# The first mixer's depthwise convolution: 32x32 products on four PSUM banks in place of 64x64 products on two

## The chip, the core and the metric

The kernel runs on one core of a Trainium2 chip. The core has a matrix engine (TensorE, PE in the rows), a vector engine (VectorE, DVE), a scalar engine (ScalarE, ACT), GpSimd (POOL, hardly used here) and SyncE (SP), whose queue issues nearly all transfers. TensorE writes into PSUM, eight banks of 128 partitions x 512 fp32 numbers; everything else lives in SBUF, with 128 partitions, or in DRAM. The metric is the time of one execution on the device in microseconds (us), lower is better.

## The reference, cut to what matters

Two residual layers and their feed-forward networks on 1024 tokens of width 1024. The first layer's mixer ("mixer 0") has two parallel parts behind one input projection: a gated depthwise causal convolution of 31 taps on 512 channels, and an mLSTM with four heads of width 128.

```python
z = h @ w_in                                   # ca, cg, q, k, v, og, gates
u = ca * jax.nn.sigmoid(cg)
u = causal_depthwise_conv(u, conv_w, conv_b)   # 31 taps, each channel by itself
u = jax.nn.silu(layernorm(u, ln_g, ln_b))
...                                            # mLSTM on q, k, v -> hm
return jnp.concatenate([u, hm], -1) @ w_out
```

Everything is float32. The large projections are done as three products of numbers split in a high and a low part; the convolution and the mLSTM use plain fp32 products, each of which the profile shows as two records.

## The kernel before, in words

**The convolution on TensorE.** The 512 channels come in four blocks of 128; block i is made by `conv_in(i)` (gate, line 378 and on) and convolved by `conv(i)` (line 393 and on). A time t is written as 8n + s: s is a phase (8 of them), n runs over 128. `conv_in` leaves u as (channel, phase, n) and stores it to DRAM (`ud[i]`, L391). `conv` loads it back with (channel, phase) on the partitions (tile `ur`, L399), with four columns of zeros ahead of n = 0 (L397). One output phase of one channel is then a sum over the 8 input phases and over five shifts of n. So a product has 8 channels x 8 phases = 64 rows, the same 64 as outputs, and 128 columns (n), and five of them (m = 0..4) add up in PSUM. The band matrices (tile `cw`, L405) are prepared on the host and are mostly zeros: 8 channels do not mix.

Sixteen blocks of 8 channels by five shifts are 80 products for each `conv(i)`. Two row halves (j: partitions 0 to 63 and 64 to 127) go to two banks, two column halves (hc) to the halves of a bank's partitions; e picks the bank's columns and the band tile. When all are done, VectorE adds the bias and moves the banks to SBUF (L417, two instructions of 512 columns).

**What surrounds it.** The mixer's program is written in the order of `ORDER0` (line 31): c0 g0 c1 c2 q0 c3 a0a v0 x0a v1 x0b g1 q1 a1a v2 x1a v3 x1b and so on. c is `conv_in`, v is `conv`, g a head's v and output gate projection (`head_vo`, its products are L174 to L176 into tile `mm`, 128x256), q a head's q and k projection (`head_qk`), a and x the mLSTM of a head in two halves of 512 tokens (`head_pre`: L595 to L609; `head_mix`: L627 to L649). A list scheduler moves instructions from this order: on each engine it takes, by priority, what is ready in its own model of time. Each engine then executes its list strictly in that order.

**PSUM.** Four banks have the tag "mm" (projections), four the tag "sm" (convolution, mLSTM, sums). A tag's banks go round in the order in which tiles are asked for in the program.

**Weights.** `weights()` (L164 to L168) loads a projection's matrix as `raw` (two buffers), rounds it on ScalarE to `wH` (L167) and takes the rest on VectorE to `wL` (L168). `wH` and `wL` have three buffers each, and the band tiles `cw` take turns in the same ones. Tile `ur` has one buffer: the load for one `conv` starts when the `conv` before it has done all its products.

## Time and profile before

| | |
|---|---|
| median of 3 runs | 2102.48 us (2101.52 to 2103.54) |
| profiled execution | 2098.65 us, span 2096.9 us |
| granted TensorE clock over the span | 0.999 |
| TensorE busy | 2076.3 us, 99% |
| VectorE, ScalarE busy | 1507.4 us (72%), 865.5 us (41%) |
| the four bursts of convolution products (L411) | from 148.89, 163.00 (two records of it at 162.00), 212.50 and 226.80 us |

How rows are read: a row of the timeline is the start in us, the length, the engine (PEld is the weight load that overlaps PE), the line, the operation, the tiles written and read, the shapes, and a count of instructions that were merged; in square brackets stands how long the engine was idle just before and what ended it. A row of windows is a stretch, its length, then for each engine its busy time and the number of instructions in the stretch, the granted clock and the share and rate of the DMA engines. "Stand" below is time in which TensorE has nothing that it may start.

### The profile page before, as it was taken

The page shows a single profiled execution, that of the slowest core. Times are in us where ns is not written, and L with a number is a line of the kernel's source. Part 1 is how long each engine was busy: PE and PEld are TensorE (multiplying, and loading weights), DVE is VectorE, ACT ScalarE, POOL GpSimd, SP SyncE. Part 2 cuts the span into 40 slices and gives each one's busy share as a digit, 9 for nine tenths or more (in the row PEclk, how much of TensorE's full clock was granted, in tenths as well). Part 3 has the DMA queues.
Part 4 walks back from the last instruction along what each step waited for, and adds up shares of the span by engine and source line. Part 5 has one row for each costly group of instructions (what it writes and reads, how often), then busy time and mean ns, then how long its engine had stood idle before and what let it go on. Part 6 is the DMA issues. An engine that isn't in the chain of part 4 may idle for free.

```text
span 2096.9 us, 28455 instructions
## 1 busy us (share of the span) xinstructions
PE 2076.3 (99%) x10687; PEld 1753.5 (84%) x10687; DVE 1507.4 (72%) x2292; ACT 865.5 (41%) x1411; POOL 2.9 (0%) x15
## 2 busy tenths in 40 slices
PE   9999999999999999999999999999999999999998
PEld 8889988888888888888899978888888888888887
DVE  7555798777776666877865677667877666677686
ACT  6212337453222222444645546644522222235553
POOL 0000000000000000000000000000000000000000
PEclk9999999999999999999999999999999999999999
DMA  4323353654443334735436543553544333374344
GB/s 163 91 97 101 107 131 121 212 183 165 164 146 102 110 102 148 270 101 148 147 125 235 195 141 119 173 191 136 196 163 163 112 115 100 102 282 136 100 126 147
DMA packets 152590, 307.36 MB, mean 147 GB/s; under 512 B 24128, under 2 KB 37312, under 8 KB 152448
## 3 DMA queue, kind: packets, MB, share of 16 engines
q1 hardware_dynamic: 152176, 305.24, 44.2%
q8 instruction: 85, 1.39, 0.3%
q14 instruction: 57, 0.47, 0.1%
q10 hardware_dynamic: 272, 0.26, 0.0%
HBM read 224.67 MB, written 80.77 MB: 146 GB/s over the span
## 4 chain that ended last, share of the span: by engine, by line
PE 95%; DVE 2%; ACT 2%; DMA 1%; issue 0%; SPq 0%; DVEq 0%; ACTq 0%
PE mm L175 20%; PE mm L174 20%; PE mm L176 20%; PE sm L176 10%; PE sm L174 10%; PE sm L175 10%; PE sm L1270 1%; PE sm L1269 1%; PE sm L1272 1%; DVE wL L168 0%; DVE bs L1057 0%; DMA rb<-rowd 0%; PE sm L1297 0%; PE sm L1258 0%; PE sm L630 0%
## 5 line engine op out<-in xcount | busy, mean ns | idle before, releaser
L175 PE MATMUL mm<-hL,wH 128*128 128x512 f32 x1356 | 530.9, 392 | 0.5 <-DVE hL L339 0.4
L176 PE MATMUL mm<-hH,wH 128*128 128x512 f32 x1356 | 529.3, 391 | 0.0
L174 PE MATMUL mm<-hH,wL 128*128 128x512 f32 x1356 | 492.4, 392 | 4.6 <-DVE wL L168 3.3
L174 PEld LDWEIGHTS mm<-hH,wL 128*128 128x128 f32 x1356 | 254.2, 188 | 60.1 <-DVE wL L168 3.4
L175 PEld LDWEIGHTS mm<-hL,wH 128*128 128x128 f32 x1356 | 254.6, 188 | 53.5 <-DVE hL L339 1.1
L176 PEld LDWEIGHTS mm<-hH,wH 128*128 128x128 f32 x1356 | 254.6, 188 | 53.0 <-issue 0.2
L175 PE MATMUL sm<-hL,wH 128*128 128x512 f32 x616 | 240.1, 390 | 0.0
L176 PE MATMUL sm<-hH,wH 128*128 128x512 f32 x616 | 239.7, 389 | 0.0
L174 PE MATMUL sm<-hH,wL 128*128 128x512 f32 x616 | 209.0, 390 | 0.0
L147 ACT ACTIVATE wH<-S 128x1024 fp32r<-128x1024 f32 x97 | 102.8, 1059 | 229.2 <-PE sm L176 212.8
L147 ACT ACTIVATE wH<-q 128x512 fp32r<-128x512 f32 x143 | 90.4, 632 | 178.8 <-PE mm L176 101.2
L147 DVE TENSOR_TENSOR wL<-q,wH 128x512 fp32r<-128x512 f32 x143 | 98.6, 690 | 70.9 <-ACT wH L147 70.3
L147 ACT ACTIVATE wH<-raw 128x1024 fp32r<-128x1024 f32 (+1 forms) x90 | 89.9, 1000 | 119.5 <-PE sm L176 66.7
L175 PE MATMUL mm<-wL,hH 128*128 128x256 f32 (+2 forms) x480 | 136.0, 285 | 2.3 <-DVE wL L168 2.3
L147 DVE TENSOR_TENSOR wL<-S,wH 128x1024 fp32r<-128x1024 f32 x97 | 118.4, 1221 | 26.2 <-ACT wH L147 26.2
L175 PEld LDWEIGHTS sm<-hL,wH 128*128 128x128 f32 x616 | 115.6, 188 | 24.7 <-issue 0.7
L174 PEld LDWEIGHTS sm<-hH,wL 128*128 128x128 f32 x616 | 115.6, 188 | 24.4 <-PE mm L176 0.5
L176 PEld LDWEIGHTS sm<-hH,wH 128*128 128x128 f32 x616 | 115.6, 188 | 24.3 <-issue 0.2
L174 PE MATMUL mm<-wH,hL 128*128 128x256 f32 (+2 forms) x480 | 135.4, 287 | 0.5 <-ACT wH L167 0.3
L176 PE MATMUL mm<-wH,hH 128*128 128x256 f32 (+2 forms) x480 | 135.6, 285 | 0.0
L1497 DVE TENSOR_TENSOR c<-sm,c 128x512 f32<-128x512 f32 x110 | 75.6, 687 | 69.7 <-PE sm L176 69.7
L147 DVE TENSOR_TENSOR wL<-raw,wH 128x1024 fp32r<-128x1024 f32 (+1 forms) x90 | 103.4, 1150 | 11.6 <-ACT wH L147 11.6
(355 smaller groups left out, 3535.1 us busy)
## 6 DMA issues: line engine op xcount, KB each, us to landing
raw<-in_w SPq DMA_DIRECT2D x108, 512.0 KB, 3.5
mdT<-c SPq DMA_DIRECT2D x88, 256.0 KB, 2.0
m<-mdT SPq DMA_DIRECT2D x88, 256.0 KB, 2.6
mdB<-c SPq DMA_DIRECT2D x66, 256.0 KB, 2.5
raw<-in_od_u SPq DMA_DIRECT2D x32, 512.0 KB, 3.9
q<-in_w SPq DMA_DIRECT2D x60, 256.0 KB, 5.3
m<-mdB SPq DMA_DIRECT2D x55, 256.0 KB, 2.8
raw<-in_ev_u SPq DMA_DIRECT2D x20, 512.0 KB, 3.3
```

Source lines behind the costliest of these rows:

```text
L147: ins = ACT.activation(dst[0], src, AF.Copy), lo.tensor_tensor(out=dst[1], in0=src, in1=dst[0], op=ALU.subtract)
L174: return (PE.matmul(o, lt[1], rt[0], start=start and not on, stop=False, skip_group_check=on), PE.matmul(o, lt[0], rt[1], start=False, sto ...
L175: PE.matmul(o, lt[0], rt[1], start=False, stop=False, skip_group_check=on),
L176: PE.matmul(o, lt[0], rt[0], start=False, stop=stop, skip_group_check=on))
L1269: PE.matmul(db[:, cc, :], kw[:, cs], v[:, c, :], start=True, stop=True)
L1270: PE.matmul(ob[:, cc, :], A[:, cs], v[:, c, :], start=True, stop=st is None)
L1272: PE.matmul(ob[:, cc, :], q[:, cs], st, start=False, stop=True)
L1497: DVE.tensor_tensor(out=out, in0=a, in1=b, op=ALU.add)
```

## The change

A product of the convolution now has 4 channels x 8 phases = 32 rows and 32 outputs. Sixteen such blocks fit on the array: four row groups r, each with its own bank, by four column groups k, each with its quarter of a bank's partitions. A `conv(i)` has 160 products where it had 80, two band tiles where it had four (half the bytes: the band matrices hold fewer zeros), four loads of `ur` with 32 partitions each where it had two with 64, and four evictions of 256 columns where it had two of 512. The four banks are two of tag "sm" and two of tag "mm". The result lands in the same places of the same tiles.

```diff
-                    for j in range(2):
-                        SP.dma_start(raw[64 * j:64 * j + 64, :, SH:],
-                                     ud[i][64 * j:64 * j + 64].rearrange("(g c) s n -> (c s) g n", g=8))
-                bs = [bank("sm") for _ in range(2)]
-                for e in range(4):
+                    for r in range(4):
+                        SP.dma_start(raw[32 * r:32 * r + 32, :, SH:],
+                                     ud[i][32 * r:32 * r + 32].rearrange("(g c) s n -> (c s) g n", g=8))
+                bs = [bank(t) for t in ("sm", "mm", "sm", "mm")]
+                for e in range(2):
                     with tc.high_priority(offset=WOFF):
-                        w = wp.tile([P, 1088], F32, tag="wL" if e % 2 else "wH", name=nm("cw"))[:, :(SH + 1) * P]
-                        SP.dma_start(w, ev_cw[4 * i + e])
+                        w = wp.tile([P, 1088], F32, tag="wL" if e else "wH", name=nm("cw"))[:, :(SH + 1) * P]
+                        SP.dma_start(w, ev_cw[2 * i + e])
                     for m in range(SH + 1):
-                        for hc in range(2):
-                            for j, b in enumerate(bs):
-                                rows = slice(64 * j, 64 * j + 64)
-                                o = (hc * (SH + 1) + m) * 64
-                                PE.matmul(b[64 * hc:64 * hc + 64, e * NT:(e + 1) * NT], w[rows, o:o + 64],
-                                          raw[rows, 2 * e + hc, m:m + NT], start=m == 0, stop=m == SH)
-                for j, b in enumerate(bs):
+                        for k in range(4):
+                            for r, b in enumerate(bs):
+                                rows = slice(32 * r, 32 * r + 32)
+                                o = (k * (SH + 1) + m) * 32
+                                PE.matmul(b[32 * k:32 * k + 32, e * NT:(e + 1) * NT], w[rows, o:o + 32],
+                                          raw[rows, 4 * e + k, m:m + NT], start=m == 0, stop=m == SH)
+                for j in range(2):
                     y = xy(2 * i + j if i < 2 else 2 * i + j - 4, int(i > 1))
                     Y.append(y)
-                    g = 8 * i + 4 * j
-                    DVE.tensor_tensor(out=by_phase(y), in0=by_phase(b), ...)
+                    for k in range(2):
+                        g = 8 * i + 4 * j + 2 * k
+                        DVE.tensor_tensor(out=y[:, 2 * k * NT:(2 * k + 2) * NT]..., in0=bs[2 * j + k][:, :2 * NT]..., ...)
...
-    band = band.reshape(16, P, 2 * (SH + 1) * 64)
+    band = band.reshape(8, P, (SH + 1) * P)
```

The scheduler also places other instructions differently around the convolutions. Lines behind the convolution are two higher in the changed kernel (L627 is now L629, L630 is L632, L633 is L635, L606 to L609 are L608 to L611).

TensorE, before, right behind the first burst of the convolution (`v_436`, `kw`, `rb`: the mLSTM of head 0; `mm`: the products of head 1, four banks of them):

```order
L411 MATMUL sm_1335<-ur_1330,cw_1402 64x128
L627 MATMUL sm_1428<-v_436,kw_1328 128x129
L628 MATMUL sm_1429<-v_436,rb_1307 128x129 x2
L174 MATMUL mm_1650<-wH_1634,hL_26_156 128x256
L174 MATMUL mm_1677<-wH_1634,hL_26_156 128x256
L174 MATMUL mm_1704<-wH_1634,hL_26_156 128x256
L174 MATMUL mm_1731<-wH_1634,hL_26_156 128x256
L627 MATMUL sm_1449<-v_436,kw_1328 128x129
L175 MATMUL mm_1650<-wL_1635,hH_25_155 128x256
```

and with the change, at the same place:

```order
L411 MATMUL mm_1339<-ur_1330,cw_1422 32x128
L629 MATMUL sm_1510<-v_436,kw_1328 128x129
L630 MATMUL sm_1511<-v_436,rb_1307 128x129 x2
L629 MATMUL sm_1531<-v_436,kw_1328 128x129
L630 MATMUL sm_1532<-v_436,rb_1307 128x129
L411 MATMUL mm_1560<-ur_1553,cw_1563 32x128 x18
L629 MATMUL sm_1510<-v_436,kw_1328 128x129
L632 MATMUL sm_1511<-st_1514,qk_1067 128x129
L411 MATMUL mm_1562<-ur_1553,cw_1563 32x128 x15
L632 MATMUL sm_1532<-st_1519,qk_1067 128x129
```

Before, 48 products of head 1 stand between the bursts of convolutions 0 and 1. With the change none does; the products of convolution 1 (`ur_1553`) on one mm bank, 18 of them, stand behind five of the mLSTM, and those of head 1 come behind all of convolution 1. Between convolutions 2 and 3 it is the same.

SP, with the change, from the last band tile of convolution 1 on (`ud<-u_1195` is the store of block 3, `ur_1553` the load for convolution 1, `raw_2032` a weight load):

```order
L405 DMA cw_1563<-in_ev_cw 128x640
L164 DMA raw_2032<-in_ev_u 128x1024
L391 DMA ud<-u_1195 128x1024
L399 DMA ur_1553<-ud 32x8x128 x4
L164 DMA raw_2038<-in_ev_u 128x1024
L591 DMA rb_2188<-rowd 128x512
```

The four loads of `ur` stand where two stood, behind the store of block 3; the weight load `raw` ahead of that store is new there, and a band tile that stood between the store and `ur` is gone.

VectorE, with the change, around the same burst (`wL_1799`: the low part of head 1's first weights; `kw_1328`: what the first mLSTM product behind the burst reads):

```order
L608 SCALAR_TENSOR_TENSOR rb_1307<-sm_1311,rb_1307 128x512
L609 SCALAR_TENSOR_TENSOR qk_1067<-qk_1067,wb_1308 128x512
L168 TENSOR_TENSOR wL_1799<-raw_1796,wH_1798 128x1024
L611 TENSOR_TENSOR kw_1328<-sm_1316,wk 128x512
L387 SCALAR_TENSOR_TENSOR t_1301<-t_1301,mm_1251 128x512
L388 SCALAR_TENSOR_TENSOR u_1195<-t_1301,rr_375 128x64x8
L418 TENSOR_TENSOR xy_198_1504<-sm_1336,col 128x256
```

Before, that L168 stood behind the first eviction (L417); now it stands ahead of `kw` and of the last step of block 3's u (L388).

## The prediction

> **What bounds the kernel now.** The page comes first, for the engine that sets the end and for how much slack it has.

> ```profile
> PE 2076.3 (99%) x10687; PEld 1753.5 (84%) x10687; DVE 1507.4 (72%) x2292; ACT 865.5 (41%) x1411; POOL 2.9 (0%) x15
> PE 95%; DVE 2%; ACT 2%; DMA 1%; issue 0%; SPq 0%; DVEq 0%; ACTq 0%
> ```

> TensorE is busy 99% of the span and the chain of waits lies 95% on it. So a microsecond taken off TensorE counts, and so does every new one in which it stands. Next the timeline of TensorE around the convolutions (start, length, engine, line, operation). They come in two pairs, convolutions 0 and 1, then 2 and 3; `x` counts records, two for each fp32 product.

> ```profile
> 147.47 1.05 PE L595 MATMUL sm<-qk,qk 128*128 128x128 f32 x8
> 148.36 0.60 PE L600 MATMUL sm<-ident,qk 128*128 128x128 f32 x4
> 148.89 4.60 PE L411 MATMUL sm<-ur,cw 64*64 64x128 f32 x160
> 153.42 0.49 PE L627 MATMUL sm<-v,kw 128*128 128x129 f32 x2
> 154.11 0.72 PE L174 MATMUL mm<-wH,hL 128*128 128x256 f32 x4
> 155.43 0.38 PE L175 MATMUL mm<-wL,hH 128*128 128x256 f32 x1 [0.38 <-DVE wL L168]
> 163.00 4.61 PE L411 MATMUL sm<-ur,cw 64*64 64x128 f32 x158
> 167.54 1.16 PE L595 MATMUL sm<-qk,qk 128*128 128x128 f32 x8
> 169.84 0.28 PE L176 MATMUL mm<-wH,hH 128*128 128x256 f32 x1
> 175.35 0.38 PE L627 MATMUL sm<-v,kw 128*128 128x129 f32 x2
> 212.50 4.60 PE L411 MATMUL sm<-ur,cw 64*64 64x128 f32 x160
> 217.03 0.49 PE L627 MATMUL sm<-v,kw 128*128 128x129 f32 x2
> 226.80 4.61 PE L411 MATMUL sm<-ur,cw 64*64 64x128 f32 x160
> 240.30 0.38 PE L627 MATMUL sm<-v,kw 128*128 128x129 f32 x2
> ```

> A burst takes 153.42 - 148.89 = 4.53 us, 28.3 ns a record; four are 18.1 us. Between the bursts of a pair TensorE runs the products of the next head (L174 to L176, tile mm, 128x256): 48 in the first pair, 45 in the second by the order of the program, 96 in each pair up to 175.35 and 240.30. From 169.84 to 175.35 stand 46 of them: 0.12 us each.

> **The burst itself.** Is it held by the array, or by the rate at which instructions come? The windows of L411 (busy, then in brackets the records that lie in the window):

> ```profile
> 148.88:148.92 0.04, 0.03 (x4) 0.03 (x4) 1.00 1.22 320
> 148.92:148.97 0.05, 0.05 (x4) 0.05 (x8) 1.00 0.64 256
> 148.97:149.04 0.07, 0.07 (x4) 0.07 (x8) 1.00 0.92 329
> 149.04:149.08 0.04, 0.04 (x8) 0.04 (x8) 1.00 0.80 320
> ```

> Four records start within 0.04 us, none in the next 0.12, then four more within 0.04. That is a round of four tiles each 4 x 28.3 = 113 ns, and the full-array product L595 takes 0.89 / 8 = 111 ns a record: each tile works as long as the whole array would, and four work side by side. Instructions come at four pairs in at most 0.04 us, sixteen in at most 0.16. The change has 320 records a burst in rounds of sixteen: 20 x 0.111 = 2.2 us at best, 20 x 0.16 = 3.2 if starts bind. I take 2.24, because the first four came in less than their window. Isolated, four bursts would save 4 x 2.3 = 9.2 us.

> [...]

> **What the new order does to the gain.** All four banks of a convolution now include two of tag mm. Banks of a tag are handed out in program order, and in that order convolution 1 (3) stands before the next head. So the next head's products can no longer slip between the bursts, as the order in the section on the change shows: after burst 0 come five products of the mLSTM, then convolution 1. Its input `ur` has one buffer and is loaded only after burst 0. What fixes its landing:

> ```profile
> 148.56 0.69 DVE L606 SCALAR_TENSOR_TENSOR rb<-sm,rb 128x512 f32<-128x512 f32 x1 [0.20 <-PE sm L595]
> 149.77 0.68 DVE L609 TENSOR_TENSOR kw<-sm,wk 128x512 f32<-128x512 f32 x1
> 151.08 1.08 DVE L388 SCALAR_TENSOR_TENSOR u<-t,rr 128x512 f32<-128x512 f32 x1
> 154.19 1.19 DVE L168 TENSOR_TENSOR wL<-raw,wH 128x1024 fp32r<-128x1024 f32 x1
> 152.19 0.33 SPq L391 DMA_DIRECT2D ud<-u  x1
> 154.24 1.27 SPq L399 DMA_DIRECT2D ur<-ud  x2
> L399 SPq DMA_DIRECT2D ur<-ud x8: 585/622/702, 52.3 to 217.8; - x8
> DMA to landing us min/median/max: 3.8/4.1/5.0
> ```

> *Pair one*, with these rows. The burst ends at 148.89 + 2.24 = 151.13. On VectorE the cut L168 now stands ahead of L609 and L388: some 1.15 us, so kw is there at 151.55 (stand 0.4) and L388 ends at 153.3. Five products at (154.11 - 153.42) / 3 = 0.23 bring TensorE to 152.7. On SP the store of convolution 3's u (L391) waits for L388 and stands ahead of the four `ur` quarters: first issue at 153.65. Quarters r0 and r1 together are the bytes of one half now, so r1, which the first waiting product needs, lands 4.1 later, 157.7: **TensorE stands 5.0 us**. The quarters' own price is in no row; the bounds are 3.8 and 5.0, so 4.7 to 5.9. Until the sm banks come free only one row group's products run, 18 and then 15, four side by side: 9 and 7.5 rounds of 0.111, 1.0 and 0.83 us. With the six mLSTM products between them (0.23 each and about 0.2 for changing over) TensorE is at 161.05. Then 40 products eight at a time (10 rounds) and 87 nearly all sixteen at a time: 2.3, so the second burst ends at 163.6, against 167.54.

> What is late next is the second half's kw:

> ```profile
> 162.10 0.33 SPq L589 DMA_DIRECT2D rb<-rowd  x1
> 165.35 0.69 DVE L602 TENSOR_TENSOR rb<-rb,mask 128x512 f32<-128x512 f32 x1 [0.97 <-DMA rb<-rowd]
> 168.34 1.23 DVE L168 TENSOR_TENSOR wL<-raw,wH 128x1024 fp32r<-128x1024 f32 x1 [2.29 <-ACT wH L167]
> 171.85 0.66 DVE L435 TENSOR_TENSOR s<-s,xy 128x512 f32<-128x512 f32 x1
> 173.62 0.55 DVE L609 TENSOR_TENSOR kw<-sm,wk 128x384 f32<-128x384 f32 x1
> ```

> The load of rb waits for the last L628 (160.6), lands 3.25 later, L168 starts 3.0 after that (166.9), takes 1.23, and kw is done 2.3 after its end: 170.4. TensorE has 1.24 of L595/L600 and 38 head products (4.55) and is there at 169.4: it stands 1.0. It starts L627 at 170.5, 4.85 earlier than 175.35, with 38 head products done and not 96: 58 x 0.12 = 6.95 are still owed. **Pair one: +2.1.** The evictions become four of 256 columns; at half of L417's 0.68 they are no dearer and lie under this chain.

> *Pair two* has no L391 in the way. VectorE has more:

> ```profile
> 212.46 0.68 DVE L606 SCALAR_TENSOR_TENSOR rb<-sm,rb 128x512 f32<-128x512 f32 x1
> 214.26 2.32 DVE L577 SCALAR_TENSOR_TENSOR qk<-z,col,qk 128x512 f32<-128x512 f32 x3
> 217.28 0.69 DVE L581 SCALAR_TENSOR_TENSOR qk<-t,qk 128x512 f32<-128x512 f32 x1 [0.70 <-ACT t L580]
> 217.89 0.68 DVE L417 TENSOR_TENSOR xy<-sm,col 128x512 f32<-128x512 f32 x1
> 220.23 0.29 DVE L633 COPY st<-sm 128x129 f32<-128x129 f32 x1
> ```

> Burst 214.74; kw 215.5 (stand 0.8); products to 216.7; first quarter at 215.2 behind a weight load that waits for L168; r1 at 219.1 (stand 2.4); 18 products to 220.1. The next L627 needs the copy L633, which stands behind L581 (1.15 later, done 219.1), four evictions (1.4) and L168 (1.2): 222.0, stand 1.9. From there products and the chain of L636 and L646 bring the second burst's end to 227.6 (now 226.80 + 4.53 = 231.3), and kw of half two to 234.3, 1.5 after TensorE has done its 33. It is 5.95 ahead of 240.30 and owes 63 x 0.12 = 7.55. **Pair two: +1.6.**

> Removed without effect: eight weight loads of 320 KB, since TensorE waits for cw in none of the rows above. From 240 us to the end of this mixer the list of waits has none of TensorE, so there is no idle time that the owed products could fill. **Sum: +3.7 us.** The profiled execution took 2098.65 (span 2096.9), 3.8 under the median; the difference is carried over: 2102.48 + 3.7 = **2106.2 us**. All my stands together are about 13 us, 5.4, 1.0, 0.8, 2.4, 1.9 and 1.5, so an error of a third in them is 4 us.

> **Rivals.**

> *The stands are short and the gain shows.* For it: the bursts do shrink, and a quarter load has half the descriptors. With the stands at a third of the above, 8.7 less: 2097.5. Against: they hang on three separate chains (DMA, VectorE, ScalarE), all rows of this trace. It turns to faster once the stands fall under about 5 us.

> *The clock falls while TensorE stands.* At the kernel's start, after idling:

> ```profile
> 1.61 3.90 PE L109 MATMUL sm<-t 128*128 128x256 f32 x10 [1.61 <-DVE t L106]
> PE mm L174 <- DVE least L1059: 2.5, 1, 2.5
> ```

> 0.39 us a record, where twice L595's 111 ns would be 0.22: a TensorE that comes from rest is 1.75 times slower. TensorE's longest wait in the trace is the 2.5 us of the last row; the new one is 5.0. If some 4 us of work after it run so, +3: 2109; in both pairs +6: 2112. [...] No row here shows a fall in mid-kernel.

> *No more than now side by side.* The columns loaded as weights are the same (160 x 64 = 320 x 32). If they bind, a record takes 14 ns and a burst its 4.5; the first bursts only fill the wait, the second ones cost about 1 to 2: 2109. If every pair of instructions keeps its 28.3 ns, a burst takes 9.06 and each pair of bursts costs some 9 more: 2124. Against both: the bunched starts.

> **How the numbers follow.** This kernel's measurement tells 0.2% (4.2 us) from no change: faster is under 2098.3, slower over 2106.7. Forecast 0.50 (own range 2102 to 2110: 0.28 same, 0.20 slower, 0.02 faster); gain shows 0.15 (0.12 faster, 0.03 same); clock 0.20 (slower); side by side 0.10 and 0.05 (0.02 same, 0.13 slower). Faster 0.14, same 0.33, slower 0.53. The range takes in the clock case, and the gain's edge, and leaves out 2124: 2097.5 to 2114.

> **What would show it.** Right: a burst of 160 products near 2.2 us; TensorE standing 4 us or more after the first burst, released by the load of ur; no mm products of 128x256 between the bursts; 128x256 spacings of 0.12 right after the stand (0.2 would be the clock). Wrong: a burst of 4.5 or 9 us; a stand under 2 us; next-head products between the bursts; or a difference that arises after 250 us, where I expect none.

## The result and the profile after

The changed kernel takes **2120.32 us** (median of five runs, 2119.36 to 2123.53), the kernel before 2101.52 us on the same chip: a ratio of 1.0092, with a 95% interval of 1.0081 to 1.0103, so 18.8 us slower. The time lies outside the predicted range of 2097.5 to 2114. The sign was the one held likeliest; the size was not: +18.8 and not +3.7.

The profiled execution took 2123.53 us (span 2121.8). About 3.0 us of its surplus arise in the first 11 us, before any changed instruction, and the four other executions have spans of 2117.6 to 2118.7, so these 3 us are put down to that one execution. In what follows they are taken off where two times are compared. The cumulated delay of the products that both kernels have rises by 10.6 us in the first pair of convolutions and by 11.8 in the second; 2.2 are won back at some 335 us, and 1.9 are lost in the second mixer. That is 22 us and not 18.8, because the profiled execution of the kernel before, 2098.65 us, lies 2.9 under its median.

First the engines and the chain of waits on the page of the changed kernel. "issue" is time in which an engine waits for nothing that the profile shows.

```profile
PE 2093.5 (99%) x11327; PEld 1766.7 (83%) x11327; DVE 1510.1 (71%) x2300; ACT 867.1 (41%) x1411; POOL 3.0 (0%) x15
PE 95%; DVE 2%; ACT 1%; DMA 1%; issue 1%; SPq 0%; DVEq 0%; ACTq 0%
```

TensorE's busy time *rises* by 17 us (2076.3 before), although each product of a convolution covers a quarter of the array that it covered before: the bursts were to lose 9 us. The list of waits of TensorE in the stretch from 145 to 260 us says where it had nothing to do:

```profile
PE mm L411 <- issue: 5.2, 3, 3.2
PE sm L411 <- issue: 3.0, 2, 1.6
PE mm L411 <- DVE s L435: 2.3, 1, 2.3
PE mm L411 <- DMA ur<-ud: 1.1, 1, 1.1
```

The two lower rows are the expected stands for `ur` (the one put down to VectorE's L435 ends with the load too: L435 was done 0.5 us earlier). The two upper rows were in nobody's working: 8.2 us inside the bursts, in five pieces, with no engine and no transfer of data to wait for. These are the gaps of what follows; counted from the last start ahead of a gap to the first behind it, they are 0.6 to 3.5 us long. The windows of L411 show the bursts (length, busy time of products and weight loads with the records in brackets, granted clock, DMA):

```profile
151.86:158.24 6.38, 4.70 (x320) 4.04 (x320) 1.00 0.43 162
167.53:174.53 7.00, 5.42 (x254) 4.80 (x254) 0.73 0.36 77
226.10:235.08 8.98, 5.41 (x320) 4.19 (x320) 0.87 0.18 62
246.00:252.83 6.83, 5.43 (x254) 4.83 (x254) 0.72 0.37 80
```

The kernel before took 4.53 us for each whole burst. Now the two whole ones take 6.38 and 8.98, and the other two 7.00 and 6.83 for 254 records, after 66 that had already run by themselves. None is near 2.2. Inside the first burst, windows of all of TensorE's products:

```profile
151.80:152.20 0.40, 0.40 (x35) 1.00 0.00 0
152.20:152.70 0.50, 0.50 (x59) 1.00 0.00 0
152.70:153.20 0.50, 0.50 (x62) 1.00 0.00 0
155.70:156.20 0.50, 0.00 (x0) 1.00 1.01 360
```

The counts take in records that reach in from the window before. The first 32 records start within 0.23 us, 7 ns apart, which is the rate of the predicted 2.24 us for 320. From there on 32 records take 0.40 to 0.47 us, 13.2 ns a record on average, and 12.8 in the steadiest stretch (64 records in 0.82 us from 152.64 on). Then, from 155.04 to 156.99, nothing starts at all. The page has two DMA queues of the kind "instruction" (packets, MB, share of the engines). This one I take for TensorE's:

```profile
q8 instruction: 90, 1.47, 0.3%
```

A packet is 16,384 bytes. There are 90 for the 22,654 records and weight loads of TensorE here, one for 252, and 85 for 21,374 in the kernel before, one for 251. One of these loads starts at 154.36, takes 1.11 us, and TensorE goes on 1.5 us after its end. The four other gaps, too, end 1.3 to 1.4 us after the end of such a load.

The clock, in windows of the same kernel:

```profile
162.00:164.00 2.00, 1.80 (x40) 1.00 1.00 261
165.00:167.00 2.00, 2.00 (x17) 0.50 0.00 0
169.00:171.00 2.00, 2.00 (x117) 0.50 0.89 147
175.00:177.00 2.00, 2.00 (x11) 0.50 0.47 134
```

It is 0.5 from 164.5 to 171.3, again from 174.8 to 178.2, and in the second pair from 232.8 to 249.8. The kernel before has a clock of 1 in these stretches.

### The profile page after: what moved, and what is told of

Read it like the earlier page. It is cut to its first block, busy times and chain, and to the rows that moved or that the text cites. A ratio compares the mean times of both kernels' runs of the same rounds, so it can differ in the third digit from the quotient of the medians.

```text
span 2121.8 us, 29730 instructions
## 1 busy us (share of the span) xinstructions
PE 2093.5 (99%) x11327; PEld 1766.7 (83%) x11327; DVE 1510.1 (71%) x2300; ACT 867.1 (41%) x1411; POOL 3.0 (0%) x15
## 4 chain that ended last, share of the span: by engine, by line
PE 95%; DVE 2%; ACT 1%; DMA 1%; issue 1%; SPq 0%; DVEq 0%; ACTq 0%
PE mm L174 20%; PE mm L175 20%; PE mm L176 20%; PE sm L175 10%; PE sm L176 10%; PE sm L174 10%; PE mm L411 1%; PE sm L411 1%; PE sm L1272 1%; PE sm L1274 1%; PE sm L1271 0%; DVE bs L1059 0%; PE sm L632 0%; PE sm L597 0%; DVE wL L168 0%
## 5 line engine op out<-in xcount | busy, mean ns | idle before, releaser
L175 PE MATMUL mm<-hL,wH 128*128 128x512 f32 x1356 | 531.9, 392 | 0.0
L176 PE MATMUL mm<-hH,wH 128*128 128x512 f32 x1356 | 530.1, 391 | 0.0
L174 PE MATMUL mm<-hH,wL 128*128 128x512 f32 x1356 | 493.6, 393 | 3.3 <-DVE wL L168 1.2
L174 PEld LDWEIGHTS mm<-hH,wL 128*128 128x128 f32 x1356 | 255.0, 188 | 58.9 <-ACT hH L338 2.4
L176 PEld LDWEIGHTS mm<-hH,wH 128*128 128x128 f32 x1356 | 255.3, 188 | 53.3 <-issue 0.2
L175 PEld LDWEIGHTS mm<-hL,wH 128*128 128x128 f32 x1356 | 255.4, 188 | 53.0 <-DVE hL L339 0.7
L175 PE MATMUL sm<-hL,wH 128*128 128x512 f32 x616 | 240.1, 390 | 0.0
L176 PE MATMUL sm<-hH,wH 128*128 128x512 f32 x616 | 239.7, 389 | 0.0
L174 PE MATMUL sm<-hH,wL 128*128 128x512 f32 x616 | 209.0, 390 | 0.0
L147 ACT ACTIVATE wH<-S 128x1024 fp32r<-128x1024 f32 x97 | 102.8, 1060 | 231.5 <-PE sm L176 215.2
L174 PE MATMUL mm<-wH,hL 128*128 128x256 f32 (+2 forms) x480 | 136.3, 287 | 0.1
L175 PE MATMUL mm<-wL,hH 128*128 128x256 f32 (+2 forms) x480 | 136.2, 285 | 0.0
L175 PEld LDWEIGHTS sm<-hL,wH 128*128 128x128 f32 x616 | 115.6, 188 | 24.6 <-issue 0.7
L176 PE MATMUL mm<-wH,hH 128*128 128x256 f32 (+2 forms) x480 | 136.0, 285 | 0.0
L174 PEld LDWEIGHTS sm<-hH,wL 128*128 128x128 f32 x616 | 115.6, 188 | 24.5 <-PE mm L176 0.5
L176 PEld LDWEIGHTS sm<-hH,wH 128*128 128x128 f32 x616 | 115.7, 188 | 24.2 <-issue 0.2
```

Source lines behind the costliest of these rows:

```text
L147: ins = ACT.activation(dst[0], src, AF.Copy), lo.tensor_tensor(out=dst[1], in0=src, in1=dst[0], op=ALU.subtract)
L174: return (PE.matmul(o, lt[1], rt[0], start=start and not on, stop=False, skip_group_check=on), PE.matmul(o, lt[0], rt[1], start=False, sto ...
L175: PE.matmul(o, lt[0], rt[1], start=False, stop=False, skip_group_check=on),
L176: PE.matmul(o, lt[0], rt[0], start=False, stop=stop, skip_group_check=on))
```

## The experiments

Two things of the change could be at fault, and each can be changed without the other: which bank a convolution takes (the *order*), and the size of its products (the *tiles*). The first four kernels take them apart. The times of the kernel before beside each lie between 2100.8 and 2101.9.

**The order alone**: 64x64 as before, second bank from mm.

```diff
-                bs = [bank("sm") for _ in range(2)]
+                bs = [bank("sm"), bank("mm")]
```

> The kernel before, its products still 64x64 on two banks, but the second bank taken from tag mm instead of sm. That gives it the changed kernel's order: the next head's products no longer come between the two bursts of a pair. Theory 'order' (the loss comes from TensorE standing for the reload of ur and for kw): the bursts stay at 4.5 us, TensorE stands in both pairs as in the changed kernel (two to four waits of 1 to 3 us, for ur and VectorE), and the time is 5 to 13 us over before, 2107 to 2115. Rival 'bursts' (the loss comes from inside the bursts of 32x32, where TensorE ran out of instructions for 0.6 to 3.5 us five times): without 32x32 products no such gap, and the time is within 3 us of before. If the clock falls with the stands alone, it falls here too (0.5 in the rows of the granted clock); if it falls with the gaps inside the bursts, it stays at 1.

Measured: 2120.3 us, 1.0089 [1.0072, 1.0106]. That is the whole loss of the change, without one 32x32 product. Windows of TensorE, then its products in the timeline:

```profile
149.10:153.63 4.53, 4.53 (x161) 1.00 0.69 235
153.63:160.70 7.07, 2.10 (x18) 0.77 0.90 242
160.70:173.18 12.48, 12.48 (x168) 0.58 0.17 45
```

```profile
160.70 3.67 PE L411 MATMUL mm<-ur,cw 64*64 64x128 f32 x30 [3.54 <-DMA ur<-ud]
166.32 3.04 PE L411 MATMUL sm<-ur,cw 64*64 64x128 f32 x26
173.18 1.16 PE L595 MATMUL sm<-qk,qk 128*128 128x128 f32 x8
```

The burst is untouched, then TensorE stands for some 5 us, the clock is 0.5 from 157.5 to 171.2, and convolution 1 costs double and more: its first 30 records start in pairs, a pair every 0.21 us at this clock, since only the mm bank is free and only two tiles work side by side where four did; the last 130 need 6.86 us, 53 ns each, for 28.3 before. Theory "order" stands, and its guess of the time (2107 to 2115) was too low: I had priced the stands but not the slow clock behind them.

**The tiles alone**: the change with all four banks from sm.

```diff
-                bs = [bank(t) for t in ("sm", "mm", "sm", "mm")]
+                bs = [bank(t) for t in ("sm", "sm", "sm", "sm")]
```

> The changed kernel with its four banks all from tag sm, so that the next head's products may come between the bursts again. Theory 'order': the wait for ur goes under these products, the bursts take what they took side by side, and the time falls under before: 2093 to 2098. Rival 'bursts': each burst still takes 6 to 9 us with gaps in which no instruction of TensorE starts and nothing is waited for; only the wait for ur goes; the four bursts cost some 10 us more than before's 18.1, so 2107 to 2115.

Measured: 2115.8 us, 1.0065 [1.0049, 1.0082]. The products of the next head are back between the bursts, nothing waits for `ur`, and still 14.0 us are lost. The windows of L411:

```profile
150.27:159.27 9.00, 5.99 (x320) 4.99 (x320) 0.96 0.33 121
169.91:178.20 8.29, 5.39 (x320) 4.58 (x320) 1.00 0.37 67
221.33:229.83 8.50, 5.72 (x320) 4.88 (x320) 1.00 0.19 64
240.55:248.55 8.00, 5.62 (x320) 4.71 (x320) 0.92 0.28 71
```

Together 33.8 us for 18.1 before: +15.7, which is the 14.0 with a little won back elsewhere. TensorE's list of waits from 145 to 260 us has 9.0 us in four gaps with nothing to wait for, and 1.9 us in two waits for VectorE's L611 inside the first burst of each pair: there the fourth sm bank is still being read. So "bursts" stands too. Each cause alone costs most or all of what both cost together; why is told below.

**Heads first**: the change with the written order moved, so that each head's products stand between the bursts.

```diff
-ORDER0 = '... v0 x0a v1 x0b g1 q1 a1a v2 x1a v3 x1b l g2 q2 ...'
+ORDER0 = '... v0 x0a g1 v1 x0b q1 a1a v2 x1a g2 v3 x1b l q2 ...'
```

> The changed kernel with its banks as they are, but the written order moved so that all of a head's products stand between convolution 0 and 1, and between 2 and 3. Theory 'order': no wait for ur is left, TensorE has its 11 us of products there, and the time is at or under before: 2093 to 2101. Rival 'bursts': the same long bursts as in the changed kernel, gaps of 0.6 to 3.5 us inside, 2107 to 2116. The clock: if waits for ur are its cause it stays at 1 here; if the gaps inside the bursts are, it falls to 0.5 behind them.

Measured: 2126.1 us, 1.0120 [1.0103, 1.0137], outside both guesses. The bursts are 6.37, 6.04, 6.99 and 7.42 us, 26.8 together, so "bursts" again: from first to last start 4.1 to 4.3 each without the gaps, where a burst of the kernel before, measured the same way, has 4.33; to that come one or two gaps of 0.4 to 2.7. But with this order the mLSTM's weighted products of q and k (`rb`, L608) come late at the end of the stage, and there it loses more than it could have won:

```profile
PE sm L630 <- DVE rb L608: 9.6, 1, 9.6
PE mm L411 <- issue: 6.1, 4, 2.5
PE sm L630 <- DVE den L644: 3.2, 1, 3.2
```

The two waits for VectorE end at 345.0 and 370.7 us, where no products of heads are left to run meanwhile (the last one starts at 329.2). As a test of the order it is spoilt; its bursts are the cleanest of all, and serve as the base of the next kernel.

**What are the gaps?** Sixteen products more at the start of the first burst of the kernel above (the first shift of convolution 0's first half is counted twice, so the output differs); all later bursts are left as they were.

```diff
-                    for m in range(SH + 1):
+                    for q, m in enumerate([0] * (i + e == 0) + list(range(SH + 1))):
...
```

> The kernel with the heads' products between the convolutions, and in convolution 0 the first shift of its first half counted twice (16 products more at the start of the first burst, 64 instructions; the result is another one). Without them the gaps came after 243 records of burst 0, 220 of burst 1, 142 and 270 of burst 2, 246 of burst 3. Theory 'fetch': the gap sits where one 16 KB block of TensorE's instructions ends, so everything behind the extra products reaches it 32 records earlier: after 243 counted with the extra ones (211 of the old), and after 188, 110 and 238, 214 in the later bursts, in which nothing was changed. Rival 'data' (a bank, a tile of weights or of ur that comes late): the gap stays with its product, after 275, 220, 142 and 270, 246.

Windows of L411 from the start of a burst to the gap, and the gap: first of "heads first", bursts 0, 1 and 3, then the same with the sixteen products more.

```profile
149.05:152.25 3.20, 3.19 (x243) 3.06 (x244) 1.00 0.13 17
152.25:154.17 1.92, 0.27 (x11) 0.01 (x1) 1.00 0.68 241
181.07:183.94 2.87, 2.86 (x220) 2.73 (x220) 1.00 0.30 78
246.86:250.09 3.23, 3.23 (x246) 3.09 (x247) 1.00 0.37 114
```

```profile
149.61:152.81 3.19, 3.19 (x243) 3.05 (x244) 1.00 0.04 14
152.81:155.00 2.19, 0.27 (x13) 0.01 (x1) 1.00 0.72 256
183.72:186.17 2.45, 2.44 (x188) 2.31 (x188) 1.00 0.22 50
188.10:189.75 1.65, 1.64 (x128) 1.53 (x128) 1.00 0.90 313
251.92:254.74 2.82, 2.80 (x214) 2.67 (x214) 1.00 0.27 60
```

Burst 0: 243 records before the gap in both, though with the extra products these are other products. Burst 1: 220 becomes 188, burst 3: 246 becomes 214, each by exactly the 32 records put in 34 and 102 us earlier. In burst 2 the gap after 270 comes after 237, and the short one after 142 is gone. In burst 1 a new gap appears 128 records behind the first, after 316: that is 256 instructions on (a record and its weight load are two). The change itself shows the same step: counted over all records of TensorE, its five gaps lie 383, 512, 128 and 383 records apart, multiples of 128 to within a record. The gaps follow the count of instructions through the program, in steps of 256, whatever product stands there. "Fetch" had foretold that; "data" falls. What TensorE waits for in a gap is in no row: that it is the load of its next instructions is my reading, from this count and from the loads that end 1.3 to 1.5 us ahead of the end of each gap in the change. (2128.4 us, one run; the time follows its base.)

**Fewer shifts**: two of five, so 64 products a convolution (three fifths of the products are left out).

```diff
-                    for m in range(SH + 1):
+                    for m in (0, SH):
```

> The changed kernel with only the first and the last of the five shifts of each convolution: three fifths of its products are left out (the result is another one), 64 products a convolution and not 160. Theory 'fetch' (the gaps inside the bursts are TensorE's queue running dry while the next 16 KB of its instructions are loaded; 256 instructions a load, a burst of 160 products is 640): 256 instructions a convolution, so at most one short gap or none, and a burst of 128 records in 1.3 to 1.8 us at the 13.6 ns a record seen after the first 32. Rival 'rate' (each record costs 20 to 28 ns on average whatever their number): 2.6 to 3.6 us a burst. The stands for ur and kw are left as they are, so the time should lie between: about 12 to 16 us under the changed kernel by 'fetch', 7 to 11 by 'rate'.

Measured: 2110.7 us, 1.0038 [1.0023, 1.0052]; 9.6 under the change. The first bursts of the pairs, 128 records each, run in 1.64 us, 12.8 ns a record, without a gap inside: by the burst it is "fetch". By the time it is "rate" (7 to 11), since TensorE then stands another 1.1 and 1.4 us for kw, and the stands for `ur` keep their slow clock (0.50 in the window from 160 to 170 us). The time was a poor measure here; the burst was the good one.

**What sets the 12.8 ns?** Two kernels change shifts 1 to 3 only: half the moving columns (half of three fifths of the products is left out), and half the weight columns (half the outputs of these shifts are left out).

```diff
+                                n = NT // 2 if 0 < m < SH else NT
...
-                                          raw[rows, 4 * e + k, m:m + NT], ...
+                                          raw[rows, 4 * e + k, m:m + n], ...
```

> The changed kernel in which shifts 1 to 3 of each convolution compute only the first 64 of the 128 columns (half of three fifths of the products is left out; the result is another one). If the array sets the 13.6 ns a record of a burst's steady part, it falls there towards 7 ns. If the supply of instructions or the weight loads do, it stays at 13 to 14 ns, the gaps stay at 0.6 to 3.5 us, and the time is the changed kernel's within 3 us.

```diff
+                                c = 16 if 0 < m < SH else 32
-                                PE.matmul(b[32 * k:32 * k + 32, ...], w[rows, o:o + 32],
+                                PE.matmul(b[32 * k:32 * k + c, ...], w[rows, o:o + c],
```

> The changed kernel in which shifts 1 to 3 of each convolution load only 16 of the 32 weight columns and compute only these 16 outputs (half the outputs of three of the five shifts are left out; the result is another one). With half the moving columns 32 records of these shifts took 0.30 us and not 0.41, while shifts 0 and 4 kept 0.41: by a line through these two, a round of sixteen is 0.10 us that does not depend on the columns, plus the 0.106 us that a product of 128 columns takes. If that 0.10 us is the loading of weights, whose length goes with their columns, 32 records take some 0.30 us here too; if it is the supply of instructions (32 in 0.10 us), they stay at 0.41. The gaps of 0.6 to 3.5 us stay in both cases, and the time is the changed kernel's within 3 us.

Windows over shifts 2 and 3 of the first half of burst 0, in which 64 records start: the change, half the moving columns, half the weight columns.

```profile
152.64:153.46 0.82, 0.82 (x90) 0.80 (x72) 1.00 0.00 0
```

```profile
149.44:150.06 0.62, 0.62 (x91) 0.62 (x76) 1.00 0.00 0
```

```profile
150.47:151.26 0.79, 0.79 (x90) 0.75 (x71) 1.00 0.00 0
```

12.8, 9.6 and 12.4 ns a record. The weight columns do not bind. The moving columns do in part: half as many save a quarter, so neither "array alone" (7 ns) nor "supply alone" (13 to 14) holds. What makes up the rest stays open: the expectation of the second kernel named the supply of instructions for this outcome, and no run shows it by itself. It matters little: the gaps are there in both (0.6 to 3.5 us, at the same counts as in the change for the first burst, 243), and the times are 2119.7 and 2125.1 (one run each; the second is 4.8 over the change where 3 was allowed).

**The stand for `ur`**: two buffers for it, in the 64x64 kernel with the changed order, and in the changed kernel.

```diff
-                    raw = mp.tile([P, 8, NT + SH], F32, tag="ur", name=nm("ur"), bufs=1)
+                    raw = mp.tile([P, 8, NT + SH], F32, tag="ur", name=nm("ur"), bufs=2)
```

> The 64x64 kernel with banks sm and mm (which alone took 2120.3, 18.6 over before) and, in addition, two buffers for ur, so that the load for convolution 1 and 3 no longer waits for the burst ahead of it. Theory 'stands and clock': of its loss, 7.1 and 5.2 us are TensorE's stands between the bursts (153.6 to 160.7, 227.7 to 232.9, with some 1 us of products in them), and the rest comes from the clock of 0.5 behind them. With ur already there the stands shrink to the waits for VectorE, under 3 us, the clock stays at 1, and the time is 2102 to 2108. Rival 'single products': the loss comes from the products of one bank that run alone (30 records of 120 ns) and from the displaced products of the next head; then it stays at 2113 to 2121.

> The changed kernel with two buffers for ur. Theory 'both' (the order costs it its stands, the bursts of 32x32 cost what they cost without any stand): the stand for ur goes, the bursts stay at 6 to 9 us with their gaps of 0.6 to 3.5 us, and the time falls only to where the kernel with four sm banks stands, 2113 to 2117. Theory 'order alone': without the stand and its clock the time falls to 2098 to 2106.

Measured: 64x64 2106.3 us, 1.0021 [1.0012, 1.0031]; 32x32 2115.6 us, 1.0061 [1.0041, 1.0081]. Windows of TensorE's first pair in each, first 64x64, then 32x32:

```profile
150.79:155.32 4.53, 4.53 (x161) 1.00 0.71 232
155.32:167.89 12.57, 12.57 (x187) 1.00 0.66 181
```

```profile
150.47:156.51 6.04, 4.72 (x322) 1.00 0.40 148
156.51:162.15 5.64, 5.64 (x101) 1.00 0.71 193
162.15:170.49 8.34, 5.00 (x247) 0.73 0.32 85
```

With 64x64 products the second buffer takes away 14.0 of 18.6 us. From the start of the first burst to the next L595 a pair takes 17.1 us for 24.1 without it, and twice 7.0 is these 14.0. What remains shows in the records: convolution 1 runs in four pieces, mostly with one bank's products, two side by side, 9.3 us together for 4.53. With 32x32 products it wins only 4.8, since the bursts are still there, and their gaps: the 0.73 in the last row is a clock of 0.5 that begins at 166.0, right behind a gap of 2.2 us, with no other stand in the 10 us ahead of it. "Both" holds, "order alone" falls.

All times together (us):

| | one buffer of ur | two |
|---|---|---|
| 64x64, banks sm and sm (before) | 2101.5 | |
| 64x64, banks sm and mm | 2120.3 | 2106.3 |
| 32x32, four banks of sm | 2115.8 | |
| 32x32, sm and mm (the change) | 2120.3 | 2115.6 |

**Could small tiles pay with fewer instructions?** A kernel of its own: `ur` holds four copies, each shifted one block further, so that one 128x32 product does four shifts and one 32x32 product the fifth; 64 products a convolution, banks and order as before. The memory for it is taken once from q and k, once from z and v (three buffers for four).

```diff
+                    raw = mp.tile([P, 32, NT + SH], F32, tag="ur", name=nm("ur"), bufs=1)
+                    for r in range(4):
+                        SP.dma_start(raw[32 * r:32 * r + 32, :, SH - r:SH - r + NT],
+                                     ud[i].rearrange("(g c) s n -> (c s) g n", g=32))
...
+                            PE.matmul(b[32 * k:32 * k + 32, e * NT:(e + 1) * NT], ws[j][:, (4 * e + k) * 32:(4 * e + k) * 32 + 32],
+                                      raw[:, 16 * j + 4 * e + k, :NT], start=e == 0, stop=False)
```

> A kernel of its own, for the question whether side-by-side products of 32 columns can pay once there are fewer of them: ur holds four copies of the input, each shifted by one block more, on its four row groups, so that one product of 128x32 does four of the five shifts, and one of 32x32 the fifth. 64 products a convolution (256 instructions, 320 before, 640 in the change), both banks of tag sm, the order of before. To make room the q and k tiles have three buffers and not four. Array time 64 records by 111/4 ns and 64 by 111/8 or 13 ns: 1.78 + 0.87 = 2.65 us a burst against 4.53, and some 0.3 for changing over. Theory 'instructions' (a burst costs by its instructions, with one gap where a 16 KB block ends at a fast stretch): bursts of 2.9 to 4.5 us, 2095 to 2102. Rival 'any small tile is slow' (the gaps come with 32x32 tiles whatever their number): 5 us and more a burst, 2104 or more. What could spoil it elsewhere: four times the bytes of ur in a load, or the missing buffer, which would show as waits for ur or qk.

> The same stacked kernel, with the room taken from the z and v tiles (three buffers and not four) instead of q and k. The bursts should be those of its twin to 0.3 us; a difference in the time is then the price of the missing buffers, not of the convolution. 2095 to 2102 by 'instructions', 2104 or more by 'any small tile is slow'.

Measured: 2112.2 (1.0051 [1.0034, 1.0068]) and 2108.6 us (1.0035 [1.0023, 1.0046]). By the time, both lie where "any small tile is slow" had put them (2104 or more); the bursts say otherwise. The four bursts of the second (the third pair of numbers is VectorE's, which does nothing on `ur` here):

```profile
148.88:151.85 2.97, 2.97 (x128) 2.57 (x128) 0.00 (x0) 1.00 0.00 0
169.62:175.08 5.46, 5.46 (x128) 4.69 (x128) 0.00 (x0) 0.50 0.18 64
220.39:223.43 3.04, 3.04 (x128) 2.57 (x128) 0.00 (x0) 1.00 0.00 0
239.55:244.26 4.71, 4.71 (x128) 4.13 (x128) 0.00 (x0) 0.60 0.19 67
```

At full clock a burst takes 3.0 us for 4.53, with no gap, 32x32 tiles among its products, in 256 instructions (320 before, 640 in the change): "any small tile is slow" falls, it is the number of instructions. Yet the time is lost again where this kernel is not better but worse: four copies of 512 KB, in pieces of 512 bytes, move at some 180 GB/s, TensorE stands 15 us in all for them, and the second burst of each pair runs at half clock.

One more tried to load the copies in long runs (u stored with zeros ahead of each row, so that a copy is one run of 16.9 KB a partition).

```diff
-                        SP.dma_start(raw[32 * r:32 * r + 32, :, SH - r:SH - r + NT],
-                                     ud[i].rearrange("(g c) s n -> (c s) g n", g=32))
+                        SP.dma_start(raw.rearrange("p g x -> p (g x)")[32 * r:32 * r + 32, :n - r],
+                                     ud[i].rearrange("c s g x -> (c s) (g x)")[:, r:])
```

> The stacked kernel (room from z and v) with its load of ur made cheaper: the stacked one before it stood 15 us ahead of convolutions 1 and 3 for four copies of 512 KB that moved at some 180 GB/s in pieces of 512 bytes, and the clock halved behind that. Here u is stored with four zeros ahead of each row of 128 and the groups of a phase side by side, so that each copy is one run of 16.9 KB a partition, read from a start one element further for each shift. If the pieces' size held the load, four copies take some 6 us at the 350 GB/s that other loads reach in the same stretch and land before the heads' products end: no stand for ur, bursts of 2.9 to 3.2 us with the clock at 1, 4 x 1.5 = 6 us saved less some 1 to 2 for changing over and for the buffers given up: 2094 to 2100. If the bytes hold it (180 GB/s whatever the pieces), the stands stay and it takes 2107 to 2112 again.

Measured: 2106.3 us, 1.0026 [1.0016, 1.0036]; 2.3 under its twin, and neither guess. The waits:

```profile
PE sm L413 <- DMA ud<-u: 9.5, 1, 9.5
PE sm L413 <- issue: 4.4, 1, 4.4
```

The stands shrink from 15 to 14 us only: the store of u is now four transfers, two issued ahead of the copies and two behind them (153.99 and 158.03 us, the copies from 156.02), and the copies still take 11 to 13 us to land. Whether these stores or the bytes hold them is not shown. No kernel here beats the one before.

## Why the prediction was wrong

**The step that failed** is the size of a burst: "I take 2.24, because the first four came in less than their window." In its place the runs show 4.1 to 4.3 us of records from the first start to the last, plus one or two gaps, 6.0 to 9.0 us in all. A burst of the kernel before is 4.33 us from the first start to the last, so even without a gap the smaller tiles gain next to nothing. Two things were wrong in the step. The rate of the first records was taken for the rate of all: it is 7 ns for the first 32 and some 13 after that. (That the first 32 were already at hand when the burst began is my reading; no run tests it.) And four records within 0.04 us in the kernel before were read as "four pairs in at most 0.04 us, sixteen in at most 0.16", though there sixteen records take four rounds of 0.11 us, and no row shows more than four in a row at that rate. The higher bound that the working itself had (3.2 us, "if starts bind") was still below what was measured, because it too came from four records.

**What no step had**: gaps that come in steps of 256 instructions. A burst of the change has 640. In the kernel before, 320 instructions take 4.53 us, 14 ns each, 256 of them 3.6 us, and no gap stands in 18.1 us of bursts. In the change, at 6.4 ns an instruction, 256 take 1.64 us, and five gaps of 0.6 to 3.5 us stand in the bursts.

**The sum, term by term.** My working gives the order alone as its +3.7 without the gain of 9.2 that was in it: +12.9. The kernel with the order alone measured +18.6. The tiles were to bring -9.2 on top of that. They measured 0.0 (2120.3 against 2120.3). So 9.2 of the miss are the bursts, and 5.7 lie in the order, about what the clock is worth there (6.2, below). This split is rough, since the working's stands belong to bursts of 2.24 us. In the changed kernel itself the stands are smaller than the working had them: for `ur` 2.3 and 1.1 us of idle time where it had 5.0 and 2.4, and for the mLSTM's operands none in the list where it had 5.6 in all. The 8.2 us of gaps and the slow clock came in their place. One slip of the working has no effect on its sum: 161.05 + 2.3 is 163.35 and not 163.6, but kw came later than that either way.

**The order** was right as a mechanism. No product of a next head runs between the bursts of a pair; TensorE stands behind the first one (4.0 and 3.6 us from its end to convolution 1's or 3's first product, products of the mLSTM included); the difference arises where it was expected, and 1.9 us of it later. What set the landing of `ur` was not the chain that I followed. These rows of the changed kernel are that chain (SyncE's and VectorE's timelines):

```profile
155.18 1.03 DVE L388 SCALAR_TENSOR_TENSOR u<-t,rr 128x512 f32<-128x512 f32 x1
156.24 0.33 SPq L391 DMA_DIRECT2D ud<-u  x1
158.42 2.48 SPq L399 DMA_DIRECT2D ur<-ud  x4
```

L388 ends at 156.2, which is the 153.3 of the prediction and the 3.0 of the start-up. But the load starts only at 158.42, right after the burst that reads the buffer has ended (158.24). With a burst of 2.24 us the store would have come last; with one of 6.4 the burst itself did. The landing, 3.8 us from that first issue, is the lower of the two bounds.

**The clock** was a rival with a chance of 0.20 and a price of +3 or +6. It was no rival but a part of the case: it falls in both pairs. In the 64x64 kernel the second `ur` buffer saves 14.0 us; of these 7.8 are TensorE's idle time between burst and load (7.07 - 2.10 and 5.17 - 2.36), and the remaining 6.2 are left for the clock, which is 0.5 for 13.7 us in each pair of the one kernel and 1 in both pairs of the other: the +6 of that rival. The row that had priced it does not show it, though: at the start of the kernel before, where a record took 0.39 us, the granted clock reads 1.00 (1.60 to 5.50 us).

**"No more than now side by side"** priced a burst at its 4.5 us of 14 ns a record. The rate without gaps is near that, some 13, though for another reason than the one given there: with half the weight columns it stays (12.4 ns for 12.8).

**Why two causes of 14.0 and 18.6 make 18.6.** In the order of the change the first burst of a pair is followed by a stand, and the second is preceded by one bank's products alone, in good part at half clock. The first burst's surplus (1.85 us in pair one) goes into the time from its end to the next convolution's first product, which is 4.0 and not 7.1 us. In the second, 64x64 products lose their neighbours and take 12.5 us with the mLSTM's between them (160.70 to 173.18); 32x32 products with their gaps take 12.3 (162.20 to 174.53). Over both pairs, from first burst to next L595 (L597 in the change), the 64x64 kernel takes 48.1 us and the change 49.4. The bursts cost the change nothing only because the order had already made room for them.

**The chances**: faster 0.14, same 0.33, slower 0.53. Slower came true, by a sum of mechanisms that I had set against each other as alternatives; a range made of single cases could not hold them together.

## What to carry to other kernels

Count instructions and not only array time: an fp32 product is four instructions here (two records and their weight loads) at 64x64 and at 32x32 alike, and the bursts of the change, with 256 of them in 1.64 us, had gaps of 0.6 to 3.5 us where the bursts of the kernel before, with 256 in 3.6 us, had none; a rate must be read over hundreds of records, not over the first few. Ask of a new bank tag or buffer what it orders: here the bank's tag alone, with the tiles unchanged, cost the whole 18.6 us. And a stand is to be priced with the clock that may fall behind it: it fell behind gaps of 2.2 and 2.4 us in two kernels here, and in the 64x64 kernel with the changed order it cost nearly as much as the stands (6.2 us, by difference, for 7.8).

## What the runs showed of the hardware that I had not expected

```profile
155.00:157.00 2.00, 0.64 (x43) 1.00 0.67 264
159.00:161.00 2.00, 2.00 (x19) 0.50 0.20 60
```

- A change from 32x32 products to full-array ones took 0.20 us between the starts of the last and the first at a clock of 1 (158.04 to 158.24 in the change) and 0.35 at 0.5 (165.17 to 165.52 there), where full-array products of the mLSTM followed each other at 0.11 at a clock of 1. From 64x64 products it was 0.20 too (153.22 to 153.42 in the kernel before). So interleaving a burst with a head's products was not free here.
